# S5 mixer of a decoder step: the rows by channel and token formed by selection matmuls

## The chip, the cores and the metric

The kernel runs on one core of a Trainium2 chip. The metric is the device time of one execution in microseconds (us). Everything below is told from the profiled execution of the kernel before, and from the order in which the two built programs place their instructions on each engine.

## The reference

One inference step of a two-layer decoder for 256 prompt tokens and 8 sample tokens of width 1024, all in float32. Each layer is FFN, mixer, FFN, with a layer norm after each. The second layer's mixer is the S5 state space: 64 groups of 16 channels, each with a complex diagonal state of 64.

```python
def s5_mixer(h, s0, prm, i):
    u = h.astype(f32).reshape(bsz, t, S5_GROUPS, S5_GROUP)
    ...
    bu_r = jnp.einsum('gpc,btgc->btgp', bbr, u)
    bu_i = jnp.einsum('gpc,btgc->btgp', bbi, u)
    ...
    pr, pi, sr, si = lax.associative_scan(combine, (a_r, a_i, bu_r, bu_i), axis=1)
    ...
    y = (jnp.einsum('gcp,btgp->btgc', prm['c_re'][i].astype(f32), sr)
         - jnp.einsum('gcp,btgp->btgc', prm['c_im'][i].astype(f32), si)
         + prm['d_skip'][i].astype(f32).reshape(S5_GROUPS, S5_GROUP) * u)
    zg = jax.nn.gelu(y.reshape(bsz, t, D_MODEL)).astype(h.dtype)
    out = (zg @ prm['w_glu_out'][i]) * jax.nn.sigmoid(zg @ prm['w_glu_gate'][i])
```

## The kernel before

Activations lie with channels on partitions: `xn` is 8 blocks of 128 channels by 264 tokens. Weights stream in as chunks of eight 128x128 blocks; SyncE issues their loads (`raw`, three buffers), ScalarE and VectorE split each into a high and a low part (`wh`, `wl`, four buffers), and each block costs three matmuls. `Stream.take` loads and splits ahead of use. The instructions of each engine run in the order in which the built program places them; the scheduler that places them may move an instruction ahead of others of the same engine when it is ready earlier.

`odd` is the S5 layer. It takes the prompt four tokens at a time: 64 chunks of four, so that the row of the rearranged input `U` is (channel of a group, token within its four) and its column is the chunk. `U` is 128 rows by 32 pairs of groups by 80 columns (8 zeros or sample tokens, 64 chunks, 8 sample tokens). Block k of `xn` gives `U[4k..4k+3]`. The loop over k = 0..7 does, for four pairs of groups a step:

- `states(k)`: 16 matmuls `f<-U,FT` into two PSUM tiles (tag A), then on VectorE four products `m`, their sum, two scans, two products `N` and a sum.
- `readout(k-1)`: 8 matmuls `py<-U,T` and 24 `py<-N,gx` or `py<-N,less`, then a gelu on ScalarE, `zu`.
- `gates(k-2)`: 16 matmuls `z<-zu,sel` back to channels on partitions, then `xh` (ScalarE) and `xl` (VectorE).
- GLU blocks on the `xh`, `xl` that are ready, dealt out by `fill`; those left over follow after the loop.

float32 matmuls with 64 rows of U or N stand in the trace twice, as two passes each.

At the entry of `odd`, `stats` (called at the end of the FFN) makes the layer norm's `rstd`; `unit(k)` multiplies block k on VectorE, ScalarE writes it with the tokens regrouped into `us`, and a DMA turns `us` into `U`: block 0 directly, blocks 1 to 7 through the DRAM tile `usd`, written and read back in four pieces. `self.ws.after` holds the weight loads back until the first read has been issued. `xn` itself is written by eight further ScalarE instructions.

PSUM tiles are taken by tag. `self.banks(mm="BBBC", ...)` lets an `mm` tile use the three banks of tag B and the one of tag C in turn, so four live at a time; in `odd` the GLU sums use them.

Of the kernel before, what the change touches and what calls it, by code (L numbers as in the profile page):

```python
# [98 lines left out]
def select():  # L99

    p, i, g = np.arange(128)[:, None, None], np.arange(4)[None, :, None], np.arange(32)[None, None, :]
    return (p == 4 * g + i).astype(np.float32)

# [115 lines left out]
class Trunk:  # L219
# [184 lines left out]
    def finish(self, ln, out):  # L404
# [15 lines left out]
        nc.vector.reciprocal(out=self.var, in_=v)  # L420
        self.new_x(split=False)
        for k in range(KD):
            if 2 <= k < 5:
                dve(out=r(k), in0=r(k), in1=self.dl, op=ALU.subtract)
            dve(out=r(k), in0=r(k), in1=self.var, op=ALU.mult)  # L425
            if k in (4, 7):
                nc.vector.tensor_scalar(out=self.xn[:, k, :], in0=r(k), scalar1=self.g(ln, k), scalar2=self.b(ln, k),
                                        op0=ALU.mult, op1=ALU.add)
            else:
                nc.scalar.activation(self.xn[:, k, :], r(k), AF.Identity, scale=self.g(ln, k), bias=self.b(ln, k))  # L430
# [44 lines left out]
    def ffn(self, layer, f, ln_in, ln_out, raw=True):  # L475
        nc = self.nc
        with ExitStack() as ctx:
# [69 lines left out]
            if ln_out < 5:  # L547
                self.stats()
            else:
                self.finish(ln_out, self.a["y"])  # L550
# [957 lines left out]
    def s5_second(self, pool, scr):  # L1508
# [7 lines left out]
        self.sel = pool.tile([128, 4, 32], F32, name="sel")  # L1516
        t_, cmul, cmul_b = self.complex(scr)
# [84 lines left out]
        with now():  # L1602
# [3 lines left out]
            nc.gpsimd.dma_start(out=self.sel, in_=a["sel"])  # L1606
        dm = cst[:, C_DM:C_DM + 64]
# [11 lines left out]
    def odd(self, ln_in, ln_out):  # L1619
# [4 lines left out]
        with ExitStack() as ctx:  # L1624
# [14 lines left out]
            us = p.tile([128, KD, 4, 80], F32, name="us")  # L1639
# [7 lines left out]
            for t in parts:  # L1647
                nc.gpsimd.memset(t[:, :, :, 0:9], 0.0)

            usd = self.dram.tile([D, 4, 80], F32, name="usd")  # L1650
            self.new_x(split=False)
            nc.gpsimd.memset(us[:, :, :, 0:8], 0.0)
            nc.gpsimd.memset(us[:, :, :, 72:80], 0.0)
            for k in range(KD):
                t = self.unit(k)
                kw = dict(scale=self.g(ln_in, k), bias=self.b(ln_in, k))
                nc.scalar.activation(us[:, k, :, 8:72], t[:, :NP].rearrange("p (c j) -> p j c", j=4), AF.Identity, **kw)
                nc.scalar.activation(us[:, k, 0, 0:8], t[:, NP:], AF.Identity, **kw)
                if k == 0:
                    nc.scalar.activation(us[:, k, 3, 72:80], t[:, NP:], AF.Identity, **kw)  # L1660
                else:
# [286 lines left out]
```

## Time and profile before

| | us |
|---|---|
| median of 3 runs (lowest, highest) | 1186.69 (1185.93, 1187.33) |
| the profiled execution's own time | 1181.86 |
| its span in the trace | 1180.1 |
| TensorE busy in the span | 1126.4 |
| VectorE busy | 881.6 |
| ScalarE busy | 590.8 |

The span is from the first to the last instruction of the profiled execution. A busy matmul engine is not an engine at its peak, since matmuls overlap. In the rows further down a time is counted from the start of the span; a row of the timeline gives start, length, engine, line, operation, tiles, shapes and count, and in brackets how long the engine was idle before it and what ended that. PE is TensorE, DVE VectorE, ACT ScalarE, SPq the queue of DMAs issued by SyncE. The length of several merged matmuls ends with the last one's latency.

### The profile page before, as it was taken

How to read it: one execution, taken by the hardware profiler on the slowest of the kernel's cores; microseconds unless marked ns; L12 is line 12 of the kernel's file. 1: busy time of each engine (PE TensorE's matmuls, PEld its weight loads, DVE VectorE, ACT ScalarE, POOL GpSimd, SP SyncE). 2: the span in 40 equal slices, each digit the busy share in tenths (PEclk: the TensorE clock that was granted, in tenths of full speed). 3: DMA queues.
4: the chain of work that ended last, by engine and by line, in shares of the span. 5: the costliest groups of instructions: out<-in, count | busy, mean ns of one | idle time of the engine just before them, and what ended most of it. 6: DMA issues, size and time to landing. Idle time of an engine off the chain costs nothing. (4 is left out here: it accounts for less than half of the span.)

```text
span 1180.1 us, 26369 instructions
## 1 busy us (share of the span) xinstructions
PE 1126.4 (95%) x10711; PEld 1067.7 (90%) x10711; DVE 881.6 (75%) x1739; ACT 590.8 (50%) x1030; POOL 176.8 (15%) x296
## 2 busy tenths in 40 slices
PE   7999999979999998999999999999969999999996
PEld 6999999977986677999999999999958899999995
DVE  4999855889875769988876797675669699555564
ACT  4544544664245565744454564454463366444442
POOL 0000000364535314010110112100020002000000
PEclk9999999989999999999999999999979999999998
DMA  7755656624565314476775567665564253655651
GB/s 250 234 168 157 211 177 207 205 89 123 158 184 151 124 53 143 135 240 215 262 233 174 156 201 228 203 182 178 175 200 154 86 192 116 208 180 182 183 178 49
DMA packets 66122, 204.96 MB, mean 174 GB/s; under 512 B 13464, under 2 KB 16616, under 8 KB 65744
## 3 DMA queue, kind: packets, MB, share of 16 engines
q1 hardware_dynamic: 56400, 174.09, 47.4%
q0 software_dynamic: 6560, 23.27, 6.2%
q10 hardware_dynamic: 3040, 5.92, 1.6%
q8 instruction: 84, 1.38, 0.5%
q14 instruction: 38, 0.31, 0.1%
HBM read 192.22 MB, written 10.86 MB: 172 GB/s over the span
## 5 line engine op out<-in xcount | busy, mean ns | idle before, releaser
L198 DVE TENSOR_TENSOR wl<-raw,wh 128x1024 fp32r<-128x1024 f32 (+2 forms) x317 | 388.5, 1227 | 184.0 <-ACT wh L197 180.9
L197 ACT CAST wh<-raw 128x1024 fp32r<-128x1024 f32 (+2 forms) x317 | 329.9, 1041 | 344.5 <-issue 100.0
L295 PE MATMUL pd<-hh,wh 128*128 128x264 f32 x704 | 200.8, 285 | 0.0
L297 PE MATMUL pd<-hh,wl 128*128 128x264 f32 x704 | 200.7, 285 | 0.0
L296 PE MATMUL pd<-hl,wh 128*128 128x264 f32 x704 | 199.1, 283 | 0.0
L295 PE MATMUL pg<-xh,wh 128*128 128x264 f32 x648 | 184.8, 285 | 3.3 <-DVE fixc L467 1.8
L297 PE MATMUL pg<-xh,wl 128*128 128x264 f32 x648 | 184.4, 285 | 1.6 <-DVE wl L198 1.5
L296 PE MATMUL pg<-xl,wh 128*128 128x264 f32 x648 | 183.6, 284 | 0.0
L297 PE MATMUL pu<-xh,wl 128*128 128x264 f32 x608 | 173.2, 285 | 2.0 <-DVE wl L198 1.9
L295 PE MATMUL pu<-xh,wh 128*128 128x264 f32 x608 | 172.9, 284 | 0.0
L296 PE MATMUL pu<-xl,wh 128*128 128x264 f32 x608 | 172.7, 284 | 0.0
L295 PEld LDWEIGHTS pd<-hh,wh 128*128 128x128 f32 x704 | 132.4, 188 | 0.6
L297 PEld LDWEIGHTS pd<-hh,wl 128*128 128x128 f32 x704 | 132.6, 188 | 0.2
L296 PEld LDWEIGHTS pd<-hl,wh 128*128 128x128 f32 x704 | 132.4, 188 | 0.0
L295 PEld LDWEIGHTS pg<-xh,wh 128*128 128x128 f32 x648 | 122.4, 189 | 4.2 <-ACT xh L451 2.0
L297 PEld LDWEIGHTS pg<-xh,wl 128*128 128x128 f32 x648 | 121.8, 188 | 2.7 <-DVE wl L198 2.7
L296 PEld LDWEIGHTS pg<-xl,wh 128*128 128x128 f32 x648 | 122.5, 189 | 0.0
L297 PEld LDWEIGHTS pu<-xh,wl 128*128 128x128 f32 x608 | 114.3, 188 | 3.0 <-DVE wl L198 2.9
L296 PEld LDWEIGHTS pu<-xl,wh 128*128 128x128 f32 x608 | 115.0, 189 | 0.0
L295 PEld LDWEIGHTS pu<-xh,wh 128*128 128x128 f32 x608 | 114.9, 189 | 0.0
L295 PE MATMUL raw<-rh,wh 128*128 128x266 f32 x192 | 56.7, 295 | 3.8 <-DVE r L346 3.7
L498 ACT CAST hh<-h 128x264 fp32r<-128x264 f32 x79 | 32.2, 409 | 55.6 <-DVE h L497 55.4
(559 smaller groups left out, 2214.6 us busy)
## 6 DMA issues: line engine op xcount, KB each, us to landing
raw<-in_w SPq DMA_DIRECT2D x308, 512.0 KB, 3.7
raw<-in_w SPq DMA_DIRECT2D x7, 384.0 KB, 5.5
gxd<-gc SPq DMA_DIRECT2D x8, 256.0 KB, 2.7
qb<-qd POOLq DMA_DIRECT2D x8, 256.0 KB, 4.5
FT<-wd POOLq DMA_DIRECT2D x8, 256.0 KB, 5.4
bF<-in_bF POOLq DMA_DIRECT2D x8, 256.0 KB, 4.4
rot<-rotd ACTq DMA_DIRECT2D x5, 384.0 KB, 5.2
rotd<-T POOLq DMA_DIRECT2D x2, 768.0 KB
```

What stands on the lines that cost most here:

```text
L197: nc.scalar.copy(wh[:, :w], raw[:, :w])
L198: nc.vector.tensor_tensor(out=wl[:, :w], in0=raw[:, :w], in1=wh[:, :w], op=ALU.subtract)
L295: mm(ps, lhsT=wh, rhs=xh, start=start, stop=False)
L296: mm(ps, lhsT=wh, rhs=xl, start=False, stop=False)
L297: self.last_mm = mm(ps, lhsT=wl, rhs=xh, start=False, stop=stop)
L498: self.last = [nc.scalar.copy(hh[:, m, :], h), self.last_mm]
```

## The change

A constant `selu` is loaded beside `sel`: for token offset j it sends channel p of a strip of 32 to row 4p + j. `rows(k)` forms `U[4k..4k+3]` with it: for each of the four strips of 32 channels (one `pu` tile in PSUM each, tag `mm`) four matmuls of 64 columns and two of 8, so 24 in all, each with 32 rows and 128 columns of weights; the four `pu` tiles are then copied to `U`, two by VectorE and two by ScalarE. `rows(0)` and `rows(1)` stand ahead of the loop, and loop steps 0, 1 and 2 form two further blocks each. `us`, `usd`, the ten DMAs and the hold on the weight loads are gone, and `xn` is written once. The layer norm ahead of it is finished as at the end of the program (`quick_stats`, `quick_unit`, cut out of `finish`) instead of by `stats`. The GLU sums of the first GLU blocks are taken from the `mm` banks only after `rows(7)`.

```diff
@@ -100,6 +100,12 @@
 
     p, i, g = np.arange(128)[:, None, None], np.arange(4)[None, :, None], np.arange(32)[None, None, :]
     return (p == 4 * g + i).astype(np.float32)
+
+
+def spread():
+
+    p, j, m = np.arange(128)[:, None, None], np.arange(4)[None, :, None], np.arange(128)[None, None, :]
+    return (m == 4 * (p % 32) + j).astype(np.float32)
 
 
 def gu(layer, f, first):
...
@@ -401,7 +407,7 @@
         for k0, k1 in ((1, 2), (2, 4), (4, 6), (6, 8)):
             self.center(k0, k1, nc.gpsimd)
 
-    def finish(self, ln, out):
+    def quick_stats(self):
 
         nc = self.nc
         dve, pool = nc.vector.tensor_tensor, nc.gpsimd.tensor_tensor
...
@@ -418,16 +424,27 @@
         for k in range(2):
             dve(out=r(k), in0=r(k), in1=self.dl, op=ALU.subtract)
         nc.vector.reciprocal(out=self.var, in_=v)
+        self.ws.hold = False
+
+    def quick_unit(self, k):
+        r, dve = self.r[:, k, :], self.nc.vector.tensor_tensor
+        if 2 <= k < 5:
+            dve(out=r, in0=r, in1=self.dl, op=ALU.subtract)
+        dve(out=r, in0=r, in1=self.var, op=ALU.mult)
+        return r
+
+    def finish(self, ln, out):
+
+        nc = self.nc
+        self.quick_stats()
         self.new_x(split=False)
         for k in range(KD):
-            if 2 <= k < 5:
-                dve(out=r(k), in0=r(k), in1=self.dl, op=ALU.subtract)
-            dve(out=r(k), in0=r(k), in1=self.var, op=ALU.mult)
+            r = self.quick_unit(k)
             if k in (4, 7):
-                nc.vector.tensor_scalar(out=self.xn[:, k, :], in0=r(k), scalar1=self.g(ln, k), scalar2=self.b(ln, k),
+                nc.vector.tensor_scalar(out=self.xn[:, k, :], in0=r, scalar1=self.g(ln, k), scalar2=self.b(ln, k),
                                         op0=ALU.mult, op1=ALU.add)
             else:
-                nc.scalar.activation(self.xn[:, k, :], r(k), AF.Identity, scale=self.g(ln, k), bias=self.b(ln, k))
+                nc.scalar.activation(self.xn[:, k, :], r, AF.Identity, scale=self.g(ln, k), bias=self.b(ln, k))
             nc.sync.dma_start(out=out[:, k, :], in_=self.xn[:, k, :])
 
     def center(self, k0, k1, e):
...
@@ -544,7 +561,9 @@
                 if first and m == KD - 2:
                     for _ in self.side:
                         pass
-            if ln_out < 5:
+            if ln_out == 3:
+                self.quick_stats()
+            elif ln_out < 5:
                 self.stats()
             else:
                 self.finish(ln_out, self.a["y"])
...
@@ -1636,7 +1657,6 @@
             for k in range(3):
                 tables(k, nc.sync)
             U = p.tile([128, Q, 80], F32, name="U")
-            us = p.tile([128, KD, 4, 80], F32, name="us")
             s_out = self.as0
             p_out = p.tile([128, Q, 2], F32, name="p_out")
 
...
@@ -1646,36 +1666,28 @@
             parts = [p.tile([128, 4, 4, 73], F32, name=f"N{i}") for i in range(2)]
             for t in parts:
                 nc.gpsimd.memset(t[:, :, :, 0:9], 0.0)
-
-            usd = self.dram.tile([D, 4, 80], F32, name="usd")
             self.new_x(split=False)
-            nc.gpsimd.memset(us[:, :, :, 0:8], 0.0)
-            nc.gpsimd.memset(us[:, :, :, 72:80], 0.0)
             for k in range(KD):
-                t = self.unit(k)
-                kw = dict(scale=self.g(ln_in, k), bias=self.b(ln_in, k))
-                nc.scalar.activation(us[:, k, :, 8:72], t[:, :NP].rearrange("p (c j) -> p j c", j=4), AF.Identity, **kw)
-                nc.scalar.activation(us[:, k, 0, 0:8], t[:, NP:], AF.Identity, **kw)
-                if k == 0:
-                    nc.scalar.activation(us[:, k, 3, 72:80], t[:, NP:], AF.Identity, **kw)
-                else:
-                    nc.gpsimd.tensor_copy(us[:, k, 3, 72:80], us[:, k, 0, 0:8])
-                if k == 0:
-
+                nc.scalar.activation(self.xn[:, k, :], self.quick_unit(k), AF.Identity, scale=self.g(ln_in, k), bias=self.b(ln_in, k))
+
+            def rows(k):
+
+                pu = [self.ps([128, 80], "pu") for _ in range(4)]
+                x = self.xn[:, k, :]
+                xj = x[:, :NP].rearrange("p (c j) -> p j c", j=4)
+                parts = [(slice(8, 72), j, xj[:, j, :]) for j in range(4)]
+                parts += [(slice(0, 8), 0, x[:, NP:]), (slice(72, 80), 3, x[:, NP:])]
+                for n, (o, j, v) in enumerate(parts):
                     for i in range(4):
-                        nc.sync.dma_start(out=U[:, i, :], in_=us[32 * i:32 * i + 32, 0])
-                elif k % 2:
-                    k0 = max(k - 1, 1)
-                    d = usd[k0 * 128:(k + 1) * 128]
-                    nc.sync.dma_start(out=d.rearrange("(k p) j t -> p k (j t)", p=128), in_=us[:, k0:k + 1].rearrange("p k j t -> p k (j t)"))
-                    read = nc.sync.dma_start(out=U[:, 4 * k0:4 * k + 4, :], in_=d.rearrange("(q g) j t -> (g j) q t", g=32))
-                    if k == 1:
-                        self.ws.after = read
-            for k in range(KD):
-                nc.scalar.activation(self.xn[:, k, :], self.r[:, k, :], AF.Identity, scale=self.g(ln_in, k), bias=self.b(ln_in, k))
+                        R = slice(32 * i, 32 * i + 32)
+                        mm(pu[i][:, o], lhsT=self.selu[R, j, :], rhs=v[R], start=n in (0, 4, 5), stop=n >= 3)
+                for i in range(4):
+                    (nc.scalar.copy if i % 2 else nc.vector.tensor_copy)(U[:, 4 * k + i, :], pu[i])
+
+            for k in range(2):
+                rows(k)
             self.new_h()
-            glu = [self.ps([128, NT], f"glu{i}") for i in range(2 * GG)]
-
+            glu = []
             pair = gelu = None
 
             def tt(o, x, y, op, e=nc.vector):
...
@@ -1783,6 +1795,11 @@
             for k in range(KD + 1):
                 if k < KD:
                     states(k)
+                if k < 3:
+                    for k2 in range(2 + 2 * k, 4 + 2 * k):
+                        rows(k2)
+                    if k == 2:
+                        glu += [self.ps([128, NT], f"glu{i}") for i in range(2 * GG)]
                 if k > 1:
                     gates(k - 2)
                     free += 2 * GG
...
@@ -1790,7 +1807,6 @@
 
                     begun = True
                     fill(4 * GG)
-                    self.ws.after = None
                 if k:
                     readout(k - 1)
             run(blocks)
```

The order of the built programs follows. In it `f` and `py` are the matmuls named above, `pu<-xn,selu` those of `rows`; a matmul stands once, and its line numbers are those of its own version. On the matmul engine, from the first `f` on, the kernel before has:

```order
L1700 MATMUL f<-U,FT 64x72 x16
L1733 MATMUL py<-U,T 64x72 x8
L1738 MATMUL py<-N_11301,gx 64x72
L1739 MATMUL py<-N_11301,less 64x72
L1740 MATMUL py<-N_11301,gx 64x72
```

The changed program has, from its first `f` (state 0) to the last of state 1:

```order
L1712 MATMUL f<-U,FT 64x72 x16
L1683 MATMUL pu<-xn,selu 128x64 x16
L1683 MATMUL pu<-xn,selu 128x8 x8
L1712 MATMUL f<-U,FT 64x72 x3
L1683 MATMUL pu<-xn,selu 128x64 x12
L1683 MATMUL pu<-xn,selu 128x8 x6
L1712 MATMUL f<-U,FT 64x72 x4
L1683 MATMUL pu<-xn,selu 128x64 x4
L1683 MATMUL pu<-xn,selu 128x8 x2
L1712 MATMUL f<-U,FT 64x72 x9
L1683 MATMUL pu<-xn,selu 128x64 x16
L1683 MATMUL pu<-xn,selu 128x8 x8
```

`rows(2)` stands between the `f` of states 0 and 1, and `rows(3)` in two pieces inside those of state 1; the last piece is its third strip alone. The waits of the built program give why: a `pu` tile waits for the copy that empties its bank, and the third strip of `rows(3)` waits for VectorE's second copy of `rows(2)`.

On the same engine, where the `f` of state 2 stand, the kernel before has the end of `py` of state 0 directly ahead of them:

```order
L1739 MATMUL py<-N_11301,less 64x72
L1740 MATMUL py<-N_11301,gx 64x72
L1700 MATMUL f<-U,FT 64x72 x16
L1753 MATMUL z<-zu,sel 32x72 x16
L1733 MATMUL py<-U,T 64x72 x8
```

The changed program has, behind `rows(4)` and ahead of the 24 `py<-N` of state 0, which the 16 `f` of state 2 follow:

```order
L1745 MATMUL py<-U,T 64x72 x3
L1683 MATMUL pu<-xn,selu 128x64 x12
L1683 MATMUL pu<-xn,selu 128x8 x6
L1745 MATMUL py<-U,T 64x72 x4
L1683 MATMUL pu<-xn,selu 128x64 x4
L1683 MATMUL pu<-xn,selu 128x8 x2
L1745 MATMUL py<-U,T 64x72
L1750 MATMUL py<-N_11302,gx 64x72
```

`rows(5)` has moved in ahead of all of `py` of state 0; three of its strips wait for VectorE's first copy of `rows(4)` at the latest, the last one for a ScalarE copy of `rows(5)` itself. At the next step the same holds with `rows(7)` ahead of `py` of state 1 and of the `f` of state 3, and there the last strip waits for VectorE's second copy of `rows(6)`.

On VectorE, from the scans of state 1 on, the kernel before has:

```order
L1715 SCALAR_TENSOR_TENSOR x<-rot,m 128x256 x2
L1682 TENSOR_TENSOR m<-f,rot 128x256
L1682 TENSOR_TENSOR N_11302<-x,rot 128x8x64 x2
L1705 SCALAR_TENSOR_TENSOR m__11499<-f,rot 128x256
L1682 TENSOR_TENSOR N_11302<-N_11302 128x4x64
```

The changed program has at the same place:

```order
L1727 SCALAR_TENSOR_TENSOR x<-rot,m 128x256 x2
L1685 COPY U<-pu 128x80
L1694 TENSOR_TENSOR N_11303<-x,rot 128x8x64 x2
L1685 COPY U<-pu 128x80
L1694 TENSOR_TENSOR N_11303<-N_11303 128x4x64
L1685 COPY U<-pu 128x80 x2
L1694 TENSOR_TENSOR m<-f,rot 128x256
```

Products of state 2 stood ahead of the `N` of state 1; now the four copies stand there, and the products of state 2 come last. Two further moves carry less: one more weight chunk is split (`wh`, `wl`) ahead of the FFN's last square, so that one split instead of two stands between states 3 and 4 on VectorE; and on SyncE three weight loads stand ahead of the six table loads (`rot`, `gx`), which were first. From the products of state 4 on, the two programs place the same work in nearly the same order.

## Rows read from the trace of the kernel before

**Rows 1.** The page's first line.

```profile
span 1180.1 us, 26369 instructions
```

**Rows 2.** Timeline, entry of the S5 layer.

```profile
866.08 0.84 ACT L1657 ACTIVATE us<-r,vec 128x256 f32<-128x256 f32 x1 [0.82 <-DVE r L446]
...
869.64 2.62 PE L1700 MATMUL f<-U,FT 64*64 64x72 f32 x30 [7.60 <-DMA U<-us]
...
872.08 0.42 DVE L1682 TENSOR_TENSOR m<-f,rot 128x256 f32<-128x256 f32 x1 [2.53 <-PE f L1700]
...
874.67 4.09 ACT L1675 ACTIVATE xn<-r,vec 128x264 f32<-128x264 f32 x8
```

**Rows 3.** Timeline, VectorE: first products of states 1, 3, 4, and a split.

```profile
880.15 0.42 DVE L1682 TENSOR_TENSOR m<-f,rot 128x256 f32<-128x256 f32 x1 [2.83 <-PE f L1700]
...
890.23 0.42 DVE L1682 TENSOR_TENSOR m<-f,rot 128x256 f32<-128x256 f32 x1
...
894.13 1.20 DVE L198 TENSOR_TENSOR wl<-raw,wh 128x1024 fp32r<-128x1024 f32 x1
...
897.92 0.41 DVE L1682 TENSOR_TENSOR m<-f,rot 128x256 f32<-128x256 f32 x1
```

**Rows 4.** Windows: length, busy PE, PEld, DVE, ACT, POOL; PEclk, DMA share, GB/s.

```profile
866.00:868.00 2.00, 0.00 (x0) 0.00 (x0) 2.00 (x4) 1.89 (x4) 1.19 (x1) 0.50 0.88 336
882.00:884.00 2.00, 2.00 (x54) 1.86 (x55) 1.97 (x4) 1.83 (x3) 0.00 (x0) 0.88 0.76 200
```

**Rows 5.** Timeline, end of the FFN: split, last L296, last square, variance, first use of gx.

```profile
857.24 1.05 ACT L197 CAST wh<-raw 128x1024 fp32r<-128x1024 f32 x1 [1.87 <-PE pd L296]
...
859.78 0.28 PE L296 MATMUL pd<-hl,wh 128*128 128x264 f32 x1
...
860.86 0.42 ACT L366 ACTIVATE sqk<-r 128x264 f32<-128x264 f32 x1
...
862.15 0.43 DVE L394 TENSOR_TENSOR rstd<-var,d 128x264 f32<-128x264 f32 x1 [1.50 <-PE var L371]
...
864.84 0.42 ACT L1722 ACTIVATE less<-gx 128x256 f32<-128x256 f32 x1 [1.71 <-DMA gx<-gxd]
```

**Rows 6.** Timeline, end of the program, where finish makes the last layer norm.

```profile
1168.90 0.43 DVE L416 TENSOR_TENSOR v<-var,d 128x264 f32<-128x264 f32 x1 [1.61 <-ACT d L411]
...
1172.41 3.65 ACT L430 ACTIVATE xn<-r,vec 128x264 f32<-128x264 f32 x6 [2.53 <-DVE r L425]
```

**Rows 7.** Timeline, TensorE: f of state 2, z of state 0.

```profile
882.75 1.16 PE L1700 MATMUL f<-U,FT 64*64 64x72 f32 x29
883.91 0.71 PE L1753 MATMUL z<-zu,sel 128*32 128x72 f32 x32
```

**Rows 8.** Timeline, ScalarE: two small copies out of PSUM.

```profile
878.65 0.25 ACT L1710 COPY fs<-f 128x32 f32<-128x32 f32 x2
```

**Rows 9.** Timeline, VectorE: the end of state 0.

```profile
875.56 1.29 DVE L1682 TENSOR_TENSOR N<-x,rot 128x512 f32<-128x512 f32 x2
...
876.89 0.43 DVE L1682 TENSOR_TENSOR N<-N 128x256 f32<-128x256 f32 x1
```

**Rows 10.** Timeline, TensorE: first and last of 41 py<-N of state 1.

```profile
886.14 0.27 PE L1740 MATMUL py<-N,gx 64*64 64x72 f32 x1 [0.33 <-DVE N L1682]
...
887.45 0.22 PE L1739 MATMUL py<-N,less 64*64 64x72 f32 x1
```

**Rows 11.** Timeline, TensorE: a GLU matmul between py matmuls.

```profile
899.26 0.28 PE L1740 MATMUL py<-N,gx 64*64 64x72 f32 x2
899.48 0.39 PE L295 MATMUL glu<-xh,wh 128*128 128x264 f32 x1
899.80 0.34 PE L1738 MATMUL py<-N,gx 64*64 64x72 f32 x2
```

**Rows 12.** Timeline, TensorE: first f of states 3 and 4.

```profile
887.51 0.22 PE L1700 MATMUL f<-U,FT 64*64 64x72 f32 x1
...
896.16 0.22 PE L1700 MATMUL f<-U,FT 64*64 64x72 f32 x1
```

More of the change, by code (lines that the diff above doesn't have):

```diff
@@ L1516, in s5_second @@
         self.sel = pool.tile([128, 4, 32], F32, name="sel")
+        self.selu = pool.tile([128, 4, 128], F32, name="selu")
         t_, cmul, cmul_b = self.complex(scr)
@@ L1606, in s5_second @@
             nc.gpsimd.dma_start(out=self.sel, in_=a["sel"])
+            nc.gpsimd.dma_start(out=self.selu, in_=a["selu"])
         dm = cst[:, C_DM:C_DM + 64]
@@ L1908, in host_inputs @@
     ins = {
-        "w": _weights(inp, order), "x": _columns(x), "cst": constants(), "sel": select(), "vec": _vectors(inp),
+        "w": _weights(inp, order), "x": _columns(x), "cst": constants(), "sel": select(), "selu": spread(), "vec": _vectors(inp),
         "lora": np.concatenate([inp["w_w2"][0], inp["w_a2"][0]]), "g2": inp["w_g2"][0],
```

## The prediction, made before the changed kernel ran

> **What bounds the kernel now.** I read the page first, then the timeline of the S5 layer's entry, VectorE's timeline through the loop, the clock by windows, and the matmul engine's timeline; last the end of the program, where the new form of the layer norm already runs. The span is 1180.1 us [rows 1], and nearly all of it is matmul work; the S5 layer is one of the places where it isn't. The first `f` starts at 869.64 after 7.60 us in which TensorE had nothing, released by the DMA that brings `U` [rows 2]. ScalarE starts writing `us` at 866.08, and its eight `xn` begin only at 874.67 and take 4.09 [rows 2]. VectorE multiplies state 0 at 872.08 [rows 2], but state 1 not before 880.15, 2.83 us idle; state 3 at 890.23 and state 4 at 897.92 [rows 3]. The pause costs clock too: TensorE is granted 0.50, its lower level of 1.2 GHz, at 866 to 868, and is back at the upper one, 2.4 GHz, only within 882 to 884 [rows 4]. So the entry loses some 20 us of matmul time, of which the change can win back a part. From state 4 on both programs place the same work in nearly the same order, and the GLU blocks behind the loop are the same, so what decides is when the products of states 3 and 4 start. I call the starts of the products of states 0 to 3 T0 to T3 and follow them.
>
> **The prices.** At full clock 29 `f` records take 1.16, so (1.16 - 0.22) / 28 = 0.034 each, two tiles side by side; 32 `z` records take 0.71, so 0.016 each, four side by side [rows 7]. The 41 `py<-N` of one state run from 886.14 to 887.45 [rows 10], 0.033 each, so all 48 take 1.57. A block of `rows` is 48 records (24 matmuls, two passes), 32 of 64 columns and 16 of 8, on four strips of 32 rows with 128 columns each. No row of this trace has that form. From below: four strips side by side, as `z`, 0.016 x 48 = 0.77. From above: none side by side, an `f` alone at 0.067, scaled by 64/72 to 0.06, 32 x 0.06 + 16 x 0.03 = 2.4. I take 0.77, since both forms of small tiles here run side by side; at half clock 1.55. The Trainium skill ("TensorE: Matmul & The Clock Gate", Part 3) says that matmuls on different row groups run together and gives 3.07 times for four strips; by that a block would take an estimated 2.4 / 3.07 = 0.78. No run shows it yet. A strip alone has no neighbour: 8 x 0.06 + 4 x 0.03 = 0.6. A GLU matmul between `py` matmuls stretches 899.26 to 899.80 [rows 11]; less the two records (0.07) that leaves 0.47 for the GLU matmul and two switches of tile form, and I take 0.18 a switch. A copy of 128x80 lies between half of the 0.25 that two of 32 columns take on ScalarE [rows 8] and the 0.43 of a 128x256 sum on VectorE [rows 9]; nearer the first, I take 0.15 on VectorE, 0.2 on ScalarE.
>
> **T0.** What goes: ScalarE's regrouping, the DMAs, POOL's small copies; all off the path once the round trip is off it. What comes: one more weight chunk is split ahead of the last square. A split waits for the matmul that frees its buffer and takes 1.05 (857.24 [rows 5]); the next buffer is freed by the FFN's last L296, which ends at 859.78 + 0.28 = 860.06 [rows 5], so I put the split at 860.1 to 861.15, and the square, 860.86 before, at 861.1 (ScalarE starts the next 0.05 early). With the copy `mu` ahead of the mean's square, the variance follows at 862.45 instead of 862.15 [rows 5]. From there to the first `xn` the end of the program takes 1172.41 - 1168.90 = 3.51 [rows 6]: 865.96. ScalarE must make `less` first, which waits for `gx`, in the trace until 864.84 [rows 5]; three weight loads now go ahead of the tables, of which the last, 524 KB at 336 GB/s [rows 4], overlaps them: I take 1.0 later, and `xn` starts at 866.2. Eight `xn` at 0.51 and another `less` end at 870.6, and only then ScalarE makes its two copies of `rows(0)`, 870.9. `rows(1)` waits for those banks, so 20 of its 24 matmuls follow, at half clock 1.3: 872.2. The `f` of state 0 stand behind it: switch 0.18, first half 16 x 0.067 = 1.07, latency 0.3: **T0 = 873.8**, 1.7 later than before (872.08). Bounds: 872.5 at full clock, 876.5 without side by side.
>
> **T1.** On VectorE the `N` of a state start 875.56 - 872.08 = 3.48 after its products, the last sum 4.81 after [rows 2, 9]. The second copy of `rows(2)` stands between, done at T0 + 5.1 with the first one ahead of it. Only then the last strip of `rows(3)` runs (0.8 between clocks), then a switch, the last `f` of the first half, latency: 6.4; the second half of `f` at half clock adds 0.3 to VectorE's own steps: T1 = T0 + 6.7 = **880.5**, about as before (880.15).
>
> **T2.** First copy of `rows(4)` at T1 + 3.65; three strips of `rows(5)`, 0.6: 4.25; latency and ScalarE's copy: 4.7; the last strip: 5.3; switch and a `py`: 5.55; the 48 `py<-N` of state 0: 7.1; half of `f` and latency, 0.8: T2 = T1 + 7.95 = **888.45**. VectorE has finished state 1 with its copies at T1 + 5.8 and idles 2.1. Before, those products were placed ahead of the `N` of state 1.
>
> **T3.** Second copy of `rows(6)` at T2 + 4.95; last strip of `rows(7)` 5.55; rest of `z`, two switches, `py<-U`: 6.55; `py<-N` 8.1; half of `f` and latency: T3 = T2 + 8.9 = **897.35**, 7.1 later than 890.23 [rows 3]. The `f` of state 3 start at 896.5, 9.0 later than 887.51 [rows 12].
>
> **The sum.** State 4 has one split less ahead of it on VectorE, 1.1 (894.13 to its follower [rows 3]): 897.92 + 7.1 - 1.1 = 903.9. On TensorE the `f` of state 4 started 896.16 - 887.51 = 8.65 after those of state 3 [rows 12], so 905.15, and 0.82 later the products, less about 0.5 of that stretch which was waiting: 905.4. The later decides: 7.5 behind. The rest keeps this lag. Selection matmuls cost nothing beyond it, hidden under VectorE's products and scans; without that cover the six blocks of the loop would cost 4.6. The profiled execution (1181.86 us with a span of 1180.1) would take 1189.4; it lies 4.8 below the median, and I add the difference to the median: 1186.69 + 7.5 = **1194.2 us**. With T0 at its lower bound (-1.3) and 0.5 less on each of the three steps it is 1191.4.
>
> **The rivals.**
> - **VectorE alone sets the pace; not slower.** If the blocks of `rows` don't hold up the `f` behind them, a state takes VectorE's 5.25 (872.08 to 877.32 [rows 2, 9]) and four copies, 5.8: T3 = 873.8 + 17.4 + 0.45 for `xl` = 891.65, and with one split less the lag is 0.3: 1187.0; with T0 at its lower bound 1185.7. For it: before, VectorE is busy without pause around 890. It decides if the `f` of state 2 are ready by T1 + 5.8, 2.1 earlier than I count. Against: 1.57 of `py<-N` and the two waits on copies stand in one queue ahead of them.
> - **The strips don't run side by side.** Then T0 is 2.7 later, T1 some 2, T2 1.2 and T3 0.3: 6.2 more, 1200.4. Against it: `z` and `f` [rows 7].
> - **The clock stays low through state 2.** Half clock doubles the strip, `py<-N` and `f` on the path of T2 (2.7) and the strip of T1 (0.4): 1197.3. For it: TensorE still waits in pieces, as before, where it rose only at 882 to 884 [rows 4]. Against: from `rows(1)` to `rows(2)` it works without a pause.
>
> **Chances.** Forecast 0.66, low clock 0.12, strips apart 0.12, VectorE's pace 0.10. A measurement tells about 0.2%, 2.4 us, from no change. Slower by more: the first three, 0.90. Within: most of the last, 0.06; faster by more, if T0 is early and VectorE's pace holds and more is won, 0.04. Range: 1190.0 (the forecast's lower end and a little of the last rival) to 1199.5 (short of the strips apart).
>
> **What would show it.** Right: no DMA between the FFN and state 0; ScalarE's eighth `xn` near 870.6; products of states 0, 1, 2, 3 near 873.8, 880.5, 888.5, 897.4; VectorE idle 2 to 3 ahead of states 2 and 3, released by `f`; a block of `rows` near 0.8 at full clock. Wrong: states 2 and 3 follow at 5.8, or T0 well below 872.5, or later states that take up the lag.

## The result, and the profile after

The changed kernel takes 1215.54 us (median), the one before 1186.31 on the same chip: ratio 1.0243, interval 1.0215 to 1.0271. The direction was right, the size was not: 29 us were lost where 7.5 were forecast. One of the changed kernel's four executions (1839.65, mean granted clock 0.555) and one of e10_groups' eight further down (1376.01, 0.750) were slow ones; the medians include them, the ratios leave them out.

The profiled execution reaches VectorE's variance `v` 6.6 us later than that of before (868.72 against 862.15). Six of these lie ahead of the FFN's end. The change does not account for them: the run e3_act below, with the same code up to there, reaches `v` at 861.41. So 24.3 of the 30.9 by which the two profiled spans differ lie behind `v`, and I count from `v` on: T0 to T3 are the starts of the products of states 0 to 3, and "end" is the end of the span, all less `v`.

VectorE's timeline after; the bracket gives how long it was idle before and what ended that:

```profile
868.72 0.43 DVE L422 TENSOR_TENSOR v<-var,d 128x264 f32<-128x264 f32 x1 [0.28 <-DVE wl L204]
...
881.95 0.42 DVE L1694 TENSOR_TENSOR m<-f,rot 128x256 f32<-128x256 f32 x1 [1.05 <-PE f L1712]
...
886.95 0.23 DVE L1685 COPY U<-pu 128x80 f32<-128x80 f32 x1
888.89 0.24 DVE L1685 COPY U<-pu 128x80 f32<-128x80 f32 x1 [1.38 <-PE pu L1683]
892.24 0.24 DVE L1685 COPY U<-pu 128x80 f32<-128x80 f32 x1 [3.11 <-PE pu L1683]
892.67 0.42 DVE L1694 TENSOR_TENSOR m<-f,rot 128x256 f32<-128x256 f32 x1 [0.19 <-PE f L1712]
...
896.34 0.21 DVE L1685 COPY U<-pu 128x80 f32<-128x80 f32 x1
...
907.19 0.42 DVE L1694 TENSOR_TENSOR m<-f,rot 128x256 f32<-128x256 f32 x1 [3.49 <-PE f L1712]
...
911.95 0.24 DVE L1685 COPY U<-pu 128x80 f32<-128x80 f32 x1
...
920.11 0.42 DVE L1694 TENSOR_TENSOR m<-f,rot 128x256 f32<-128x256 f32 x1 [4.31 <-PE f L1712]
```

States 1, 2 and 3 start at 892.67, 907.19 and 920.11, that is 10.7, 14.5 and 12.9 after the one before (forecast 6.7, 7.95, 8.9; compare [rows 3]). VectorE waits each time for `pu` or `f` (1.38 and 3.11 ahead of state 1, 3.49 and 4.31 ahead of states 2 and 3), so the time is TensorE's. Its timeline shows where:

```profile
873.28 2.74 PE L1683 MATMUL pu<-xn,selu 32*128 32x64 f32 x48 [5.01 <-ACT xn L1671]
...
877.90 2.85 PE L1683 MATMUL pu<-xn,selu 32*128 32x64 f32 x42 [0.39 <-ACT U L1685]
...
886.13 2.75 PE L1683 MATMUL pu<-xn,selu 32*128 32x64 f32 x36
888.81 0.74 PE L1712 MATMUL f<-U,FT 64*64 64x72 f32 x8
889.48 2.72 PE L1683 MATMUL pu<-xn,selu 32*128 32x64 f32 x12
...
896.86 3.23 PE L1683 MATMUL pu<-xn,selu 32*128 32x64 f32 x36
...
900.70 2.72 PE L1683 MATMUL pu<-xn,selu 32*128 32x64 f32 x12
...
903.52 0.32 PE L1745 MATMUL py<-U,T 64*64 64x72 f32 x1
906.29 0.27 PE L1712 MATMUL f<-U,FT 64*64 64x72 f32 x1
...
907.58 1.54 PE L1683 MATMUL pu<-xn,selu 32*128 32x64 f32 x48
...
910.83 3.58 PE L1683 MATMUL pu<-xn,selu 32*128 32x64 f32 x48 [1.08 <-DVE U L1685]
```

A whole block of 48 records takes 2.74 at 873.28 and 1.54 at 907.58. Three strips (36 records) take 2.75, and one strip alone (12 records) still 2.72: 0.227 a record instead of 0.057. The upper clock of 907.58 and the lower one around it show in the windows (the columns are the length, the busy time of PE, PEld, DVE, ACT and POOL with their instructions, then TensorE's granted clock, the share of the DMA engines, and GB/s; PEld is the weight loads of TensorE):

```profile
873.20:905.00 31.80, 30.92 (x393) 29.64 (x395) 14.48 (x39) 7.01 (x27) 0.00 (x0) 0.50 0.11 41
905.00:910.00 5.00, 4.75 (x136) 4.47 (x133) 2.75 (x7) 2.78 (x8) 0.00 (x0) 0.86 0.38 109
910.00:915.00 5.00, 4.17 (x56) 3.95 (x58) 2.91 (x9) 0.84 (x4) 0.00 (x0) 0.82 0.08 29
915.00:920.00 5.00, 5.00 (x86) 5.00 (x85) 0.50 (x2) 0.99 (x4) 0.00 (x0) 0.50 0.00 0
920.00:930.00 10.00, 9.87 (x222) 9.07 (x219) 7.92 (x17) 3.02 (x10) 0.00 (x0) 1.00 0.34 91
```

TensorE is busy 30.92 of 31.80 us and stays at 0.50, the level of 1.2 GHz, for all of it; behind the `py<-N` of state 0 it rises, and within `rows(7)` (by the mean of 0.82, some 3.2 behind 910) it falls once more. In the kernel before it was back within 882 to 884 [rows 4], some 20 after `v`; here it is there for good 51 after.

### The profile page after: what moved, and what is told of

It is laid out like the page before. It is cut to its first block, busy times and chain, and to the rows that moved or that the text cites. A ratio compares the mean times of both kernels' runs of the same rounds, so it can differ in the third digit from the quotient of the medians.

```text
span 1211.0 us, 27124 instructions
## 1 busy us (share of the span) xinstructions
PE 1161.0 (96%) x11095; PEld 1100.9 (91%) x11095; DVE 883.6 (73%) x1759; ACT 585.1 (48%) x1029; POOL 173.9 (14%) x287
## 5 line engine op out<-in xcount | busy, mean ns | idle before, releaser
L301 PE MATMUL pi<-xh,wh 128*128 128x264 f32 x160 | 52.2, 326 | 6.4 <-DVE fixt L486 3.8
```

Of the source, the lines that this page charges most:

```text
L301: mm(ps, lhsT=wh, rhs=xh, start=start, stop=False)
```

## The experiments

The theory: TensorE's queue sets the pace of states 0 to 3, since a record of `rows` costs a weight load of 128 columns, since strips that wait for a late copy run alone, and since this work leaves the clock low. The rivals: VectorE's copies set the pace; the place of `py` in the queue does; the low clock alone does. Beside these runs the kernel before takes 1178 to 1179 (beside the changed kernel 1186), so the ratios compare. The expectations of e1_ahead to e4_late give times on the scale of the changed kernel's 1215.54, and count T0 to T3 from the FFN's last `r`, 2.5 ahead of `v`. The start of state 2 in the kernel before, which no earlier row shows, is

```profile
883.82 0.40 DVE L1682 TENSOR_TENSOR m<-f,rot 128x256 f32<-128x256 f32 x1
```

Each kernel's T0 to T3 and end come from one execution; the ends of the changed kernel and of e15_stats, which differs from it only in the layer norm ahead, are 2.0 apart.

| kernel | T0 | T1 | T2 | T3 | end | median | ratio to before (interval) |
|---|---|---|---|---|---|---|---|
| before | 9.9 | 18.0 | 21.7 | 28.1 | 318.0 | | 1 |
| changed | 13.2 | 24.0 | 38.5 | 51.4 | 342.3 | 1215.54 | 1.0243 (1.0215 to 1.0271) |
| e3_act (A) | 13.3 | 21.2 | 32.5 | 39.5 | 329.0 | 1192.55 | 1.0117 (1.0100 to 1.0134) |
| e12_load | 13.6 | 21.5 | 33.4 | 40.7 | 331.5 | 1192.73 | 1.0125 (1.0110 to 1.0140) |
| e1_ahead | 18.9 | 32.3 | 37.8 | 43.5 | 332.7 | 1194.16 | 1.0134 (1.0117 to 1.0151) |
| e4_late | 13.2 | 23.9 | 31.8 | 45.1 | 338.2 | 1200.85 | 1.0171 (1.0130 to 1.0213) |
| e2_warm | 13.2 | 23.9 | 39.1 | 53.7 | 344.4 | 1204.99 | 1.0209 (1.0184 to 1.0234) |
| e5_k128 | 26.4 | 49.6 | 76.7 | 99.3 | 389.1 | 1251.18 | 1.0629 (1.0612 to 1.0647) |
| e7_double | 13.5 | 26.7 | 43.4 | 60.4 | 351.2 | 1212.93 | 1.0300 (1.0283 to 1.0318) |
| e9_dense | 14.5 | 22.4 | 31.1 | 38.2 | 328.9 | 1192.34 | 1.0124 (1.0106 to 1.0143) |
| e8_pairs | 11.2 | 16.5 | 21.6 | 28.2 | 319.0 | 1180.55 | 1.0020 (1.0007 to 1.0033) |
| e13_pairsdve | 10.9 | 16.0 | 21.2 | 27.7 | 317.2 | 1178.34 | 1.0001 (0.9991 to 1.0010) |
| e14_pairsfill | 9.4 | 14.5 | 19.7 | 27.7 | 316.9 | 1177.37 | 0.9998 (0.9987 to 1.0009) |
| e15_stats | 13.1 | 23.8 | 38.9 | 53.4 | 344.3 | 1204.95 | 1.0222 (1.0205 to 1.0239) |
| e6_early | 14.4 | 22.3 | 34.2 | 41.8 | 332.5 | 1195.28 | 1.0153 (1.0136 to 1.0170) |
| e10_groups | 9.4 | 17.0 | 20.5 | 29.7 | 319.1 | 1182.98 | 1.0037 (1.0021 to 1.0053) |
| e11_groupsfill | 8.3 | 15.3 | 19.5 | 28.7 | 319.7 | 1181.39 | 1.0027 (1.0013 to 1.0040) |
| h1_block1 | 9.9 | 17.4 | 21.9 | 27.0 | 318.8 | 1179.25 | 1.0010 (0.9998 to 1.0022) |

**e3_act, called A: no strip alone.**

```diff
-(nc.scalar.copy if i % 2 else nc.vector.tensor_copy)(U[:, 4 * k + i, :], pu[i])
+nc.scalar.copy(U[:, 4 * k + i, :], pu[i])
```

> All four copies of a block go to ScalarE, none to VectorE; in the built order each block of rows then stands in one piece on TensorE and no strip alone. Theory (single strips cost as much as a block): 2.7 less in each of the steps to T1 and T2 and some 2 in that to T3, so T3 falls from 53.9 to about 46.5: about 1208 us. If VectorE's copies and the waits behind them set the pace, the states follow at VectorE's 5.3: T3 about 32 to 34, about 1194. If single strips are cheap in truth (their length in the trace only a wait), T3 falls by no more than the copies' own 0.9 a step: about 1213.

Half of the loss went (1.0243 to 1.0117): T1 2.8, T2 6.0 and T3 11.9 earlier. Counted as in the expectation, T3 is 42.0, between the theory's 46.5 and the 32 to 34 of VectorE's pace, so this run alone does not decide between them; e12_load does. TensorE's timeline of A has only whole blocks, at the two clocks as before, and the clock is back 31.5 after `v` instead of 51:

```profile
878.84 2.81 PE L1683 MATMUL pu<-xn,selu 32*128 32x64 f32 x48
...
894.25 1.54 PE L1683 MATMUL pu<-xn,selu 32*128 32x64 f32 x48
```

```profile
865.40:892.90 27.50, 25.27 (x414) 24.48 (x416) 12.94 (x28) 8.98 (x39) 0.00 (x0) 0.51 0.14 52
892.90:905.00 12.10, 12.10 (x328) 11.47 (x326) 9.53 (x21) 5.84 (x24) 0.00 (x0) 0.99 0.38 112
```

**e12_load: VectorE's time given back to A.** TensorE's order is A's.

```diff
+                for i in range(2):
+                    nc.vector.tensor_tensor(out=junk, in0=junk, in1=U[:, 4 * k + 2 * i:4 * k + 2 * i + 2, :].rearrange("p q t -> p (q t)"), op=ALU.add)
```

> As A, but VectorE does two more sums of 128x160 behind each block (into a tile that nobody reads), at the places where the changed kernel has its copies; TensorE's order is A's, no strip alone. Theory (the 13 us by which the changed kernel ends later than A come from the single strips that the late VectorE copies leave, not from VectorE's time): the end within 1.5 of A's 329.0 after v. Rival (VectorE's extra work ahead of the products delays the states): 0.5 to 0.9 more a state, the end 3 or more later than A's.

1.0125 against A's 1.0117: within the intervals the same. In the one trace T3 is 1.2 later and the end 2.5, between the theory's 1.5 and the rival's 3. Most of the added work VectorE absorbs in its waits for `f`, as ahead of state 2:

```profile
887.77 0.76 DVE L1689 TENSOR_TENSOR junk<-junk,U 128x160 f32<-128x160 f32 x2 [1.24 <-ACT U L1687]
892.28 0.42 DVE L1698 TENSOR_TENSOR m<-f,rot 128x256 f32<-128x256 f32 x1 [3.76 <-PE f L1716]
```

The two sums take 0.76 for a block where the changed kernel's two copies take 0.4 to 0.5. So of the 13.3 that A's end gained, at most 2.5 is VectorE's time; the rest went with the single strips, and with the low clock, which outlasts them in the changed kernel (51 after `v` against 31.5).

**e1_ahead: all blocks ahead of the loop.**

```diff
-            for k in range(2):
+            for k in range(KD):
                 rows(k)
...
-                if k < 3:
-                    for k2 in range(2 + 2 * k, 4 + 2 * k):
-                        rows(k2)
```

> All eight blocks of rows stand ahead of the loop, none in it; no strip runs alone. Times count from the FFN's last r; in the changed kernel T0 is 15.7 and T3 53.9. Theory (TensorE's queue sets the pace of states 0 to 3, by blocks of 2.7 at the lower clock and by single strips that take as long as a block): the six moved blocks delay T0 by 6 x 2.7 to about 32, then the states follow at VectorE's 5.3 to 5.8, T3 about 49, 5 earlier than in the changed kernel: about 1210 us. If an unbroken run of strip matmuls lifts the clock, blocks fall to 1.3 after the first few, T0 is 24 to 26, T3 42, about 1203. Rival (the copies on VectorE set the pace, wherever the matmuls stand): the 16 copies of the moved blocks still cost VectorE only 3 to 4, T0 near 20 and T3 near 37, about 1198.

The `f` of state 0 stand in pieces between the moved blocks, so T0 is 18.9, but T1 is 32.3; from there the states follow at 5.5 and 5.7, VectorE's pace. Counted as in the expectation, T0 is 21.4, near the rival's 20, and T3 46.0, between the theory's 49 and the rival's 37; that T1 waits for the moved blocks is the theory's. The clock did not rise over six blocks of selection matmuls, in which TensorE was busy without a pause from 866.6 on:

```profile
862.00:893.70 31.70, 30.84 (x501) 29.56 (x503) 14.02 (x40) 7.50 (x29) 0.00 (x0) 0.50 0.11 40
893.70:900.00 6.30, 5.41 (x158) 5.16 (x156) 5.75 (x12) 3.14 (x10) 0.00 (x0) 0.90 0.39 106
```

**e4_late: rows written behind readout.**

```diff
-                if k < 3:
-                    for k2 in range(2 + 2 * k, 4 + 2 * k):
-                        rows(k2)
...
                 if k:
                     readout(k - 1)
+                if k < 3:
+                    for k2 in range(2 + 2 * k, 4 + 2 * k):
+                        rows(k2)
```

> In a loop step the two blocks of rows are written behind readout instead of ahead of it, so py of state 0 stands ahead of rows(4), and rows(5) runs in two pairs of strips among the f of state 2. Theory (the amount of strip work in TensorE's queue ahead of f counts, not the place of py): T2 as before or up to 1 earlier, T3 within 2 of 53.9: 1213 to 1216 us. Rival (my prediction's step for T2: py<-N with two waits on copies ahead of the f is what delays them): T2 and T3 each about 3 earlier, about 1210 us.

T2 and T3 came 6.7 and 6.3 earlier, twice the rival's 3; my theory, which gave the place of `py` no weight, was wrong here. Order counts, and partly through the clock: behind `py<-N` it rises, `rows(4)` takes 1.54, and then it falls again, near 894.6, although TensorE was busy for all of the 14.80 us of the last two windows. So it does not take a pause to make it fall.

```profile
865.30:886.50 21.20, 19.86 (x268) 19.08 (x270) 10.24 (x29) 6.27 (x21) 0.00 (x0) 0.50 0.17 65
886.50:893.50 7.00, 7.00 (x155) 6.72 (x152) 5.10 (x13) 3.04 (x9) 0.00 (x0) 0.91 0.34 96
893.50:901.30 7.80, 7.80 (x127) 7.44 (x126) 5.13 (x12) 0.94 (x5) 0.00 (x0) 0.57 0.01 2
```

**e2_warm: TensorE's pause filled.**

```diff
+            with self.tc.issue_after(self.last_mm.ins):
+                for _ in range(26):
+                    mm(pw, lhsT=warm[:, :128], rhs=warm, start=True, stop=True)
```

> 26 matmuls of 128x512 on zeros, whose result nobody reads, fill TensorE's pause between the FFN's last matmul and the first block of rows; nothing else changes. Theory that the low clock is a cause of its own: the clock stays at its upper level, blocks and single strips take 1.25 instead of 2.7, T0 is 2 earlier, T1-T0 6, T2-T1 8.5, T3-T2 9, so T3 falls from 53.9 to about 38: about 1199 us. Rival (matmuls of 32 or 64 rows do not hold the clock up, so it falls again a few us after the fill): T0 2 earlier, the rest as in the changed kernel, about 1213.

The rival's forecast came out, but for T0. The fill and `rows(0)` ran at 1.00; then the clock fell while `rows(1)` waited 0.82 between two of its pieces, and stayed down through unbroken work. T3 is 2.3 later than the changed kernel's, about as in e15_stats (2.0):

```profile
865.00:867.00 2.00, 1.73 (x49) 1.56 (x49) 1.58 (x6) 1.45 (x4) 0.00 (x0) 1.00 0.97 386
867.00:868.80 1.80, 1.00 (x12) 0.82 (x12) 0.02 (x1) 1.80 (x6) 0.00 (x0) 0.93 0.13 46
868.80:871.60 2.80, 2.76 (x36) 2.75 (x36) 0.24 (x1) 0.10 (x2) 0.00 (x0) 0.50 0.00 0
...
873.70:879.70 6.00, 6.00 (x92) 5.81 (x90) 4.54 (x10) 0.72 (x4) 0.00 (x0) 0.50 0.01 3
```

T0 did not move, where 2 earlier was expected: `rows(1)` waits for ScalarE's copies, which stand behind the eight `xn`. As the clock was not held up, this run does not tell what the low clock costs.

**e5_k128: A with 128 rows in each selection matmul.** `selu` is laid out anew, so that a slice of it selects from all 128 channels.

```diff
-                        R = slice(32 * i, 32 * i + 32)
-                        mm(pu[i][:, o], lhsT=self.selu[R, j, :], rhs=v[R], ...)
+                        c = 128 * i + 3 - j
+                        mm(pu[i][:, o], lhsT=self.selu[:, c:c + 128], rhs=v, ...)
```

> As the run with all copies on ScalarE (call it A; its clock is 0.50 from the first block to 28 us later, T0 13.25, T3 39.5 and the end 329.0 after VectorE's v), but each selection matmul takes all 128 rows instead of a strip of 32; count, columns and results are the same. A record then should take 0.06 at full clock (two dl records of 264 columns take 0.44, 64 columns a quarter of one's 0.22), so a block 2.7 to 2.9 at full clock and twice that at half. Theory (work in strips of 32 rows leaves the clock at its lower level): the clock rises during the first blocks, a block takes 2.7 to 2.9, f and py run at the upper level, and the end is within 3 of A's. Rival (the clock stays low after the pause whatever the tile's form): a block takes 5.5 or more, six of them in the loop make the end 15 to 25 later than A's.

The strips of 32 rows are not what keeps the clock low: with full tiles it stays at 0.50 for 68 us of almost unbroken work. And the price was far off: a block takes 10.41 where 5.5 or so was expected at that clock, 0.217 a record, nearly as the single strip (0.227); the end is 60 later than A's, where the rival had 15 to 25.

```profile
887.41 10.41 PE L1683 MATMUL pu<-xn,selu 128*128 128x64 f32 x48
```

```profile
864.15:932.15 68.00, 67.44 (x362) 66.75 (x364) 12.93 (x28) 10.64 (x40) 0.00 (x0) 0.50 0.06 21
```

**e7_double: A with the matmuls of blocks 2 to 7 done twice.**

```diff
-                for n, (o, j, v) in enumerate(parts):
+                for n, (o, j, v) in list(enumerate(parts)) * (2 if k > 1 else 1):
```

> As A, but the 24 selection matmuls of blocks 2 to 7 are each done twice (the second time from the start, so the result is the same). Theory (strip work at the lower clock in TensorE's queue is on the path of every state from 1 to 4): 6 x 2.7 = 16 later at the end than A, T1 5.4 later, T2 and T3 by 11 and 16. Rival (part of it lies under VectorE's work): less than 8 later.

T1, T2 and T3 are 5.5, 11.0 and 20.9 later, the end 22: nothing of the added work is hidden. It is more than 16 because the clock comes back later still: it rises 43 after `v`, against 31.5 in A, and falls once more from 50 to 60 after.

**e8_pairs: A with two blocks under one weight load.** Each of the 24 matmuls moves 128 or 16 columns, so the eight blocks need half the matmuls, weight loads and copies.

```diff
-                x = self.xn[:, k, :]
+                x = self.xn[:, k0:k1, :]
...
-                        mm(pu[i][:, o], lhsT=self.selu[R, j, :], rhs=v[R], ...)
+                        mm(pu[i][:, :, o], lhsT=self.selu[R, j, :], rhs=v[R], ...)
```

> As A (copies on ScalarE; blocks of 48 records in 2.74 at the lower clock, end 329.0 after VectorE's v), but each selection matmul serves two blocks: 128 and 16 columns under one load of the same 32x128 weights, so half as many matmuls with the same columns in all. Theory (a record of rows costs its weight load of 128 columns beside its 64 moved ones, and four strips share that): a pair of blocks takes 3.7 to 4.1 at the lower clock instead of 5.5, four pairs save 6, the end 323, about 1186 where the kernel before takes 1178. Rival (the moved columns alone count): a pair takes 5.3 to 5.5, no change to A beyond 1.

The end is 319.0, 10 earlier than A's where the theory had 6. A pair takes 2.85 at the lower clock, hardly more than one block (2.74) and less than the theory's 3.7, and 2.43 at the upper, where a block takes 1.54: there the moved columns count too.

```profile
865.93 2.85 PE L1683 MATMUL pu<-xn,selu 32*128 32x128 f32 x48 [5.45 <-ACT xn L1671]
870.62 2.27 PE L1711 MATMUL f<-U,FT 64*64 64x72 f32 x32 [1.83 <-issue]
...
876.45 2.43 PE L1683 MATMUL pu<-xn,selu 32*128 32x128 f32 x48
```

The clock is back at 874.6, 13.7 after `v`, where A needs about 31.5:

```profile
865.90:874.60 8.70, 6.83 (x110) 6.62 (x113) 3.93 (x11) 4.49 (x13) 0.00 (x0) 0.50 0.31 119
874.60:893.00 18.40, 18.09 (x436) 16.98 (x434) 17.10 (x36) 7.64 (x32) 0.00 (x0) 1.00 0.25 74
```

**e9_dense: A with the fill and wide matmuls ahead of blocks 1 to 5.**

```diff
+                if 0 < k < 6:
+                    for i in range(4):
+                        mm(pu[i], lhsT=warm[:, :128], rhs=warm, start=True, stop=True)
```

> As A, with the fill of e2 in the pause and four more matmuls of 128x512 on zeros ahead of the selection matmuls of each of the blocks 1 to 5 (each 0.22 at the upper clock, 0.9 a block; the results are overwritten). Theory (the lower clock is a cause of its own, since selection matmuls let it fall and do not raise it): the clock stays at its upper level through the loop's start, blocks take 1.54 and f and py<-N half of what they take in A; 2.7 x 5 + 4 = some 12 less, 4.5 of added work: the end 5 to 8 earlier than A's. Rival (the clock falls in spite of the added matmuls, or does not matter): the added work at the lower clock costs 1.8 a block, the end 7 to 9 later than A's.

Neither forecast came out: the end is A's (328.9 against 329.0). The pieces tell more. Ahead of T1 the clock is back at its upper level, and blocks take 1.54; the step to T2 is 8.7 instead of A's 11.3 although it holds two groups of added matmuls (1.1 each from their start to that of the next work). So the low clock costs about 5 in that step (11.3 - 8.7 + 2.2), and the price of raising it this way eats the gain.

```profile
879.32 1.54 PE L1693 MATMUL pu<-xn,selu 32*128 32x64 f32 x48
...
884.79 1.20 PE L1684 MATMUL pu<-warm 128*128 128x512 f32 x4
```

**e13_pairsdve and e14_pairsfill: pairs, with the first pair's copies on VectorE, then with the fill as well.**

```diff
-            rows(0, 2)
+            rows(0, 2, nc.vector.tensor_copy)
```

> As the run with pairs of blocks (T0 11.2, T1 16.5, T2 21.6, T3 28.2, end 319.0 after v), with the copies of the first pair on VectorE, so that they do not wait behind ScalarE's eight xn. If these copies are what holds T0 (TensorE idles 1.8 between the first pair and f): T0 to T3 all 1.4 earlier, the end 1.4 earlier, ratio to the kernel before 1.0005 to 1.001. Rival (from state 3 on TensorE's work decides, and an earlier T0 is only idled away): T0 earlier, T3 unchanged.

> As e13_pairsdve, with the fill of 26 matmuls in TensorE's pause. The clock then is at its upper level for the first pair and, if the pair's wider matmuls hold it (in the run with pairs it came back after the second pair), for all behind it: T0 another 1 earlier, T1 to T3 1 to 2 earlier, ratio 0.998 to 1.000. Rival: it falls again within the first states, T3 unchanged.

Ratio 1.0001 and 0.9998: as fast as before, no faster. In e13_pairsdve the end is 1.8 earlier than in e8_pairs, T0 to T3 only 0.3 to 0.5 where 1.4 was expected; TensorE waits 0.44 between pair and `f` instead of 1.83:

```profile
867.95 2.31 PE L1711 MATMUL f<-U,FT 64*64 64x72 f32 x32 [0.44 <-issue]
```

In e14_pairsfill T0 to T2 are 1.5 earlier still, T3 is not: the clock falls to 0.81 and 0.76 in the windows from 20 to 28 after `v`.

**e15_stats: the changed kernel with the old finish of the layer norm.**

```diff
-            if ln_out == 3:
-                self.quick_stats()
-            elif ln_out < 5:
+            if ln_out < 5:
```

> The changed kernel with the layer norm finished as before (stats and unit) instead of the new way. Theory (the new finish is no part of the loss): v and what follows it move by less than 1, T0 to T3 and the end within 2 of the changed kernel's, ratio to the kernel before 1.022 to 1.026. Rival (the moved weight loads and the split ahead of the square delay less, xn and so T0, and the loss begins there): T0 1.5 or more earlier, the end too.

The same as the changed kernel within the intervals (1.0222 against 1.0243), and in the trace 2.0 later at the end, not earlier: the new finish is no part of the loss.

**e6_early: a failed edit.**

```diff
             for k in range(KD):
                 nc.scalar.activation(self.xn[:, k, :], ...)
+                if k < 2:
+                    rows(k)
```

> As A, but the xn of blocks 2 to 7 are written behind rows(0) and rows(1), so that ScalarE's copies of rows(0) do not wait for eight xn. Theory (T0 hangs on these copies): rows(1) follows rows(0) at once, T0 is 1.4 earlier, and the end 1.4 earlier as well, since TensorE's queue sets the rest. Rival (T0 is set by TensorE's strip work, the copies only wait in its shade): T0 moves by less than 0.4.

ScalarE still copies `rows(0)` behind all eight `xn` in the trace (871.03, where the last `xn` ends at 871.12), so the edit did not test what it was for; T0 is 1.2 later, with a wait of 1.74 for `gx` among the `xn` (0.55 in A).

**e10_groups, e11_groupsfill, h1_block1: other divisions.** Blocks 0, 1 to 3 and 4 to 7 as groups, without and with the fill; and the kernel before with block 1 alone on TensorE.

```diff
+            rows(0, 1, nc.vector.tensor_copy)
...
+                if k == 0:
+                    rows(1, 4)
+                if k == 2:
+                    rows(4, KD)
```

> Blocks in groups that share a weight load: block 0 alone (copies on VectorE), blocks 1 to 3 behind the f of state 0, blocks 4 to 7 behind the f of state 2. Theory (what matters is how much TensorE work stands ahead of each state's f): T0 near 9.5 after v, T1 near 17, T2 near 22.5, T3 near 29, as in the kernel before (9.9, 18.0, 21.7, 28.1); the group of four takes 3 to 6. The end within 2 of before's: ratio 0.999 to 1.003. Rival (the selection work must be paid in full at the end, since TensorE has no idle time from state 3 on): T0 to T3 as said, but the end 4 to 6 later than before's, ratio 1.004.

> As e10_groups, with the fill of e2 in the pause ahead of block 0. If the fill keeps the clock at its upper level over block 0 and the first f: T0 about 1.5 earlier than e10_groups, T1 2 to 3 earlier, the end 1.5 to 3 earlier; ratio to the kernel before 0.997 to 1.000. If the clock falls again during the group of three: T0 earlier, the rest unchanged.

```diff
+                if k == 1:
+                    nc.scalar.activation(self.xn[:, k, :], t, AF.Identity, **kw)
+                    continue
...
+                if k == 0:
+                    rows(1)
```

> The kernel before, with block 1 alone formed by selection matmuls behind the f of state 0 (copies on ScalarE); block 0 and blocks 2 to 7 still go through memory, and xn of block 1 is written in place of its us. Theory: VectorE's wait of 2.83 ahead of state 1 goes, T1 is 2 to 2.8 earlier, and as VectorE is busy from there on, the end too: 0.2 per cent faster than before. Rival (the transfers of the later blocks or the low clock set the next states): T1 earlier, T3 unchanged, no difference to before, or slower by the 0.9 that the block's first matmuls put ahead of f(0).

In all three T0 to T2 are near or ahead of before's, and none is faster at the end. e10_groups, at 1.0037, ends between its theory and its rival; in e11_groupsfill the fill brings T0 to T3 1.0 to 1.7 forward and nothing at the end (1.0027, where 0.997 to 1.000 was expected). h1_block1 wins 1.1 at T3 (27.0) and has lost it at state 4 (35.9 after `v`, 35.8 before): no difference to before, as its rival said.

## Why the prediction was wrong in size

- **What bounds, and the direction.** Right: no DMA stands between the FFN and state 0, VectorE idles ahead of states 2 and 3 (3.49 and 4.31), released by `f`, and the lag at state 3 (23.3) is kept to the end (24.3).
- **The prices failed.** The step "from below: four strips side by side, as `z`, 0.016 x 48 = 0.77" took records with 32 weight columns (`z`) for records with 128. Measured: 1.54 at the upper clock, inside the bounds of 0.77 to 2.4 and twice the value taken, and 2.74 at the lower for 1.55. e5_k128 and e8_pairs show what the price does not hang on at the lower clock: a record of 128 rows costs what one of 32 rows costs alone, and one with twice the moved columns costs nearly the same. No run changes the columns of the weights alone, but `py<-N`, with 64 of them instead of 128, takes half as long: 48 records in 2.77, two side by side, are 0.115 each against 0.227, though each moves 72 columns. That points to the weight load. The Trainium skill has this in "TensorE: Matmul & The Clock Gate", section "LDWEIGHTS (loading the stationary operand)": the load's time goes by its columns, and 32 rows load no faster than 128. The trace agrees for the whole record (0.227 with 32 rows and 0.217 with 128), and I had not weighed it.
- **The strip alone failed most.** 0.6 was forecast (0.8 in T1, 0.6 in T2 and T3), 2.72 measured. The order that I had read from the built program gave its place correctly; the copies it waits for also came when forecast (the copy at T1 + 3.65 at T1 + 3.67). In T2 three strips took 3.23 for 0.6, the single one 2.72 for 0.6, and `py<-N` 2.77 for 1.57 (903.52 to 906.29): 5.9 of the 6.6 by which that step was short. In T1 the single strip began 2.3 after its bank was free (886.95 + 0.23, against 889.48), behind three strips and eight `f`, and took 2.72 for 0.8. In T3 the copy came when forecast (911.95 + 0.24, T2 + 5.0 for 4.95), the last strip ended at 914.41, 1.7 late, and at the clock that had fallen again the `z`, `py` and `f` behind it took 5.7 for 3.35: together the 4.0 by which that step was short.
- **The clock.** The rival "stays low through state 2" came true and at a higher price than its 3.1, since the strips it doubles were longer; its sum also left out the three strips of `rows(5)`, and that the clock falls again ahead of state 3 stood nowhere. The argument against it, that TensorE "works without a pause", was the error: in e1_ahead and e5_k128 the clock stays at 0.50 without a pause.
- **T0** was 1.9 late (13.2 after `v`; the forecast's own was 873.8 - 862.45 = 11.35): 42 records of `rows(1)` took 2.85 for 1.3, and ScalarE's last `xn` ended 9.0 after `v` instead of 8.1 (875.15 + 2.59, behind a wait of 0.60 for `gx`).
- **The other rivals.** VectorE's pace fell with the steps of 14.5 and 12.9, against its 5.8, and with e12_load. The strips do run side by side: 10.41 / 2.74 = 3.8 times. That is more than the 3.07 quoted from the Trainium skill ("TensorE: Matmul & The Clock Gate", Part 3), which the page measured with 512 moved columns.

The loss, by ratios: 1.0243 - 1.0117 = 1.3% went with the single strips, 1.0117 - 1.0020 = 1.0% with half of the matmuls, weight loads and copies, 0.2% with the copies behind ScalarE's `xn`; by the ends of the traces 13.3, 10.0 and 1.8. The first two hold what the low clock costs, which no run takes apart in full; in one step of A it is about 5 (e9_dense). What is left equals the kernel before.

Still open: what TensorE must be doing to get its clock back. In these traces it rose behind runs of `py<-N`, in selection matmuls of 128 columns (e8_pairs) or in fills (e9_dense), and stayed low through blocks of 64 columns. But A kept the upper clock through `rows(6)` and `rows(7)`, and e14_pairsfill lost it in a pair of 128 columns. A pause is not needed for the fall, as e4_late shows; whether the long weight load or the few moved columns keep the clock low, no run separates.

## What to carry to other kernels

Price a small matmul by its weight load too: by the columns of its weights, and by whether neighbours on other rows run beside it. Before splitting tile copies over two engines, ask which strip is left alone when one engine frees its bank late; here one engine for all copies won half of the loss back. When several blocks use the same weights, move them under one load.

## What the runs showed that I had not expected

- At the lower clock 48 records with 128 moved columns took 2.85, with 64 columns 2.74; at the upper 2.43 and 1.54. The upper clock takes 44% off the time of one form and 15% off the other.
- TensorE stayed at 0.50 for 68 us while it was busy 67.44 of them (e5_k128), and in e4_late its clock fell in the midst of unbroken work.
